# Two-layer hybrid decoder trunk on one core: the mixer's gate, branch, output and recurrence key/query products stream the high and the low input part as one 512-column operand

## The chip, the cores and the metric

The kernel runs on one core of a Trainium2 chip. The metric is device time in microseconds (us). TensorE does matmuls and writes PSUM banks of 128 x 512 float32, of which a core has eight; VectorE (DVE in the profile), ScalarE (ACT) and GpSimd (POOL) do the rest; each works through its own queue in the order in which the program was written for it. The profile gives one execution, engine by engine.

## The reference

Two layers over 256 tokens of width 1024, batch 1, float32. In each layer:

```
x <- x + 1/2 * SwiGLU(RMSNorm(x))
h  = RMSNorm(x);  h @ w_in -> columns for
     A: dilated window attention, 3 head groups merged by softmax-denominator weights
     B: sliding-window grouped-query attention with per-head sinks
     C: gated linear attention (recurrence), with key, query, value, low-rank gate
     G: sigmoid gates, one of width 1024 per branch
x <- x + (sum_i G_i * (branch_i @ w_branch[i])) @ w_out
x <- x + 1/2 * SwiGLU(RMSNorm(x))
```

## The kernel before, in words

**Products.** A float32 product is made of three products of `float32r` parts: weight and input are each split into a high part (a cast) and a low part (the rest), and w_high x_high + w_high x_low + w_low x_high are summed in PSUM. A *unit* is a piece of weights of some 1024 values per partition, as a rule eight 128 x 128 blocks. It arrives by DMA; `emit_split` casts it on ScalarE to `hi` (L191), and VectorE subtracts to get `lo` (L192). `chunk()` hands out the next unit and has the split of the unit four places on written just before; `hi` and `lo` have five buffers each, so the split of unit u+5 waits until TensorE has read unit u.

**Two forms of a feature-major product.** `mm3` makes three matmuls of 256 columns for each block (L331 to L333) into half a PSUM bank. `mmw`, in use in the two SwiGLU halves of a layer, streams high and low input side by side: one 512-column matmul with the high weights for each of the eight blocks (L341), then one 256-column matmul each with the low weights (L343), into a whole bank. `joined` then adds the halves: ScalarE copies the right one to SBUF (`low`, L347), VectorE adds the left (L348).

**The mixer**, stage by stage. (1) *Start*: `tok_proj(272)` makes B's keys and values, into two banks (`psb`). Then come four units by `mm3`: the recurrence's key (two, in one bank) and query (two, in another). Meanwhile `end_norm` turns the sum of squares (L315) by L316 and a power on GpSimd (L256) into the norm's factor `n.r`, spread over partitions by L324; `psb` is read with that factor, and the keys' own norm needs two more powers. (2) Twelve 512-wide `tok_proj` for A, B and C. (3) *Gates*: 24 units by `mm3`, between which `fill()` steps two generators, attention and recurrence. The last big steps of attention are `merge` (three head groups joined; it ends in L781) and B. (4) *Branches*: 12 units by `mm3`, each into one bank, times a gate (L1033), added up (L1035), split to `mh` and `ml` (L1037, L1038). (5) *Output*: 8 units by `mm3`, added to x (L1047).

PSUM has two sets of four banks in rotation: `mm` for these products, `at` for transposes, scores and the norm. `schedule_with_timeline_sim` lets a scheduler decide, before the run, in which order each engine's instructions stand.

Of the kernel before, what the change touches and what calls it, by code (L numbers as in the profile page):

```python
# [17 lines left out]
P = 128  # L18
T = 256
# [52 lines left out]
def trunk_kernel(ctx, tc, x, positions, norm_ffn1, w_ffn1_in, w_ffn1_out, norm_mix, w_in, a_q_norm, a_k_norm,  # L72
# [127 lines left out]
    def chunk():  # L200
        u = cur[0]
        cur[0] += 1
        ahead(u)
        return splits.pop(u)
# [122 lines left out]
        nc.scalar.copy(n.rbc, ps[:, 256:512])  # L327
        yield

    def mm3(ps, wh, wl, xh, xl, first, last):  # L330
        nc.tensor.matmul(ps, wh, xh, start=first, stop=False)  # L331
        nc.tensor.matmul(ps, wh, xl, start=False, stop=False)  # L332
        nc.tensor.matmul(ps, wl, xh, start=False, stop=last)  # L333

    def mmw(ps, w, xhl, first, last):


# [174 lines left out]
    def mixer(l, n, nxt):  # L512
# [32 lines left out]
                    fill()  # L545
            return ps

        def feat_proj(o):
            wh, wl = chunk()
            for k in range(KD):  # L550
                mm3(o, wh[:, k, :], wl[:, k, :], n.h[k], n.l[k], k == 0, k == KD - 1)

        def rope(ps, t, tab, nh):
            C, S = tab
# [148 lines left out]

        yT = [[None] * 4 for _ in range(3)]

        def feature_major(i, y, t):
            pt = turned(y, 4)
            if t == 0:
                yT[i] = [big(F32R), big(F32R), big(F32R), big(F32R)]
            for e in range(2):  # L710
                hv = v3(yT[i][e], 2)[:, :, t * P:(t + 1) * P]
                lv = v3(yT[i][2 + e], 2)[:, :, t * P:(t + 1) * P]
                src = v3(pt[:, e * 256:(e + 1) * 256], 2)
                nc.scalar.copy(hv, src)
                nc.vector.tensor_sub(lv, src, f(hv))


        og = [[None] * NT for _ in range(3)]
# [43 lines left out]
        def merge():  # L762
# [31 lines left out]
            yT[0] = [big(F32R), big(F32R), big(F32R), big(F32R)]  # L794
            for e in range(2):
                nc.scalar.copy(yT[0][e], ysum[e])
                nc.vector.tensor_sub(yT[0][2 + e], ysum[e], f(yT[0][e]))
            yield

        def b_stats(t):  # L800
# [152 lines left out]

        psb = tok_proj(272, 4, True)
        next(fin)
        ps = bank("mm")
        feat_proj(ps[:, 0:T])
        next(fin)
        nc.vector.scalar_tensor_tensor(r64, n.r, 1.0 / HD, n.r, op0=OP.mult, op1=OP.mult)
        nc.vector.tensor_scalar(r8, n.r, 0.125, None, op0=OP.mult)  # L960
# [6 lines left out]
            gt.append(g)  # L967
        bv = v_side(psb, P, P)
        bk = k_rope(psb, tabs[3], 2)
        feat_proj(ps[:, T:2 * T])  # L970
        ck = big()
        nc.vector.tensor_mul(v3(ck, 2), v3(ps, 2), rb2)
        ps = bank("mm")
        for j in range(2):
            feat_proj(ps[:, j * T:(j + 1) * T])
        cq = big()
        nc.vector.scalar_tensor_tensor(v3(cq, 2), v3(ps, 2), HD ** -0.5, rb2, op0=OP.mult, op1=OP.mult)
        bkT = turn_all(bk, 2)
        streams["gla"] = gla(gt, ck, cq)
        streams["att"] = attention()  # L980
# [26 lines left out]

        gates = []
        for c in range(3 * KD // 2):
            ps = bank("mm")  # L1010
            for j in range(2):
                feat_proj(ps[:, j * T:(j + 1) * T])
                fill()
            g = big()
            nc.vector.tensor_mul(v3(g, 2), v3(ps, 2), rb2)
            nc.scalar.activation(g, g, AF.Tanh, scale=0.5)
            gates.append(g)
        while streams:
            for name in list(streams):
                step(name)  # L1020
        mh, ml = [], []
        for mp in range(KD // 2):
            acc = gates[mp]
            for i in range(3):
                wh, wl = chunk()
                ps = bank("mm")
                for j in range(2):
                    for k in range(4):
                        sl = slice((k % 2) * T, (k % 2) * T + T)
                        mm3(ps[:, j * T:(j + 1) * T], wh[:, k, j * P:(j + 1) * P], wl[:, k, j * P:(j + 1) * P],  # L1030
                            yT[i][k // 2][:, sl], yT[i][2 + k // 2][:, sl], k == 0, k == 3)
# [4 lines left out]
            h, lo = big(F32R), big(F32R)  # L1036
            nc.scalar.copy(h, acc)  # L1037
            nc.vector.tensor_sub(lo, acc, f(h))  # L1038
            mh.append(h)
            ml.append(lo)  # L1040
        for m in range(KD):
            wh, wl = chunk()
            ps = bank("mm")
            for k in range(KD):
                sl = slice((k % 2) * T, (k % 2) * T + T)
                mm3(ps[:, 0:T], wh[:, k, :], wl[:, k, :], mh[k // 2][:, sl], ml[k // 2][:, sl], k == 0, k == KD - 1)
            nc.vector.scalar_tensor_tensor(xT[m], ps[:, 0:T], 0.5, xT[m], op0=OP.mult, op1=OP.add)  # L1047
            nxt(m)


# [48 lines left out]
```

## Time and profile before

| | us |
|---|---|
| median of 3 runs (1453.31 to 1454.25) | 1454.0 |
| the profiled execution | 1454.26 |
| its span, first to last instruction | 1452.1 |
| TensorE busy in it | 1440.7 (99%) |
| VectorE busy | 1046.4 (72%) |
| ScalarE busy | 834.6 (57%) |
| GpSimd busy | 127.1 (9%) |

The profiled execution is 2.2 us longer than its span and 0.3 us above the median. A matmul's row shows its way through the array too, so rows of neighbours overlap; what a matmul costs in a stream is the distance from start to start.

### The profile page before, as it was taken

How to read it: one execution, taken by the hardware profiler on the slowest of the kernel's cores; microseconds unless marked ns; L12 is line 12 of the kernel's file. 1: busy time of each engine (PE TensorE's matmuls, PEld its weight loads, DVE VectorE, ACT ScalarE, POOL GpSimd, SP SyncE). 2: the span in 40 equal slices, each digit the busy share in tenths (PEclk: the TensorE clock that was granted, in tenths of full speed). 3: DMA queues.
4: the chain of work that ended last, by engine and by line, in shares of the span. 5: the costliest groups of instructions: out<-in, count | busy, mean ns of one | idle time of the engine just before them, and what ended most of it. 6: DMA issues, size and time to landing. Idle time of an engine off the chain costs nothing.

```text
span 1452.1 us, 23326 instructions
## 1 busy us (share of the span) xinstructions
PE 1440.7 (99%) x9098; PEld 1285.9 (89%) x9098; DVE 1046.4 (72%) x1919; ACT 834.6 (57%) x1436; POOL 127.1 (9%) x108
## 2 busy tenths in 40 slices
PE   8999999999999999999999999999999999999998
PEld 6888898888899998888888888988888999988887
DVE  6887667888677687776677766688766857777753
ACT  6565456556757456565466555466467564566542
POOL 2030012223200000000000000131220000000000
PEclk9999999999999999999999999999999999999999
DMA  9665564443452565655555655643444426565651
GB/s 294 213 198 172 170 212 146 145 145 117 146 174 75 171 220 177 201 177 179 196 194 183 195 168 170 210 152 124 146 145 146 145 88 204 175 203 175 199 182 54
DMA packets 214702, 246.31 MB, mean 170 GB/s; under 512 B 6524, under 2 KB 183376, under 8 KB 214592
## 3 DMA queue, kind: packets, MB, share of 16 engines
q1 hardware_dynamic: 214016, 243.48, 51.4%
q0 software_dynamic: 544, 1.33, 0.4%
q8 instruction: 71, 1.16, 0.3%
q14 instruction: 39, 0.32, 0.1%
q10 hardware_dynamic: 32, 0.01, 0.0%
HBM read 243.76 MB, written 1.05 MB: 169 GB/s over the span
## 4 chain that ended last, share of the span: by engine, by line
PE 95%; DVE 2%; ACT 1%; POOL 1%; DMA 1%; issue 0%; SPq 0%; DVEq 0%
PE p L341 30%; PE p L343 16%; PE p L332 6%; PE p L333 6%; PE p L331 6%; PE p L543 6%; PE p L541 5%; PE p L542 5%; PE p L686 2%; PE p L650 2%; PE p L487 1%; PE p L485 1%; PE p L486 1%; PE p L579 1%; PE p L694 1%; PE p L861 1%
## 5 line engine op out<-in xcount | busy, mean ns | idle before, releaser
L191 ACT CAST hi<-raw 128x1024 fp32r<-128x1024 f32 (+3 forms) x468 | 483.2, 1036 | 489.5 <-PE p L341 271.0
L192 DVE TENSOR_TENSOR lo<-raw,hi 128x1024 fp32r<-128x1024 f32 (+3 forms) x468 | 562.8, 1206 | 266.5 <-ACT hi L191 260.5
L341 PE MATMUL p<-a,hi 128*128 128x512 f32 x1936 | 491.0, 394 | 2.2 <-ACT hi L191 2.1
L341 PEld LDWEIGHTS p<-a,hi 128*128 128x128 f32 x1936 | 348.8, 189 | 65.5 <-ACT hi L191 2.5
L343 PEld LDWEIGHTS p<-a,lo 128*128 128x128 f32 x1936 | 265.4, 190 | 19.3
L343 PE MATMUL p<-a,lo 128*128 128x256 f32 x1936 | 272.1, 282 | 0.0
L333 PE MATMUL p<-a,lo 128*128 128x256 f32 x768 | 218.8, 285 | 0.0
L332 PE MATMUL p<-a,hi 128*128 128x256 f32 x768 | 218.3, 285 | 0.0
L331 PE MATMUL p<-a,hi 128*128 128x256 f32 x768 | 217.7, 285 | 0.0
L256 POOL TENSOR_TENSOR s<-s,neghalf 128x8 f32<-128x8 f32 (+2 forms) x42 | 94.7, 2254 | 1052.6 <-DVE s L316 708.8
L543 PE MATMUL p<-hi,a 128*128 128x512 f32 (+1 forms) x416 | 162.1, 392 | 0.0
L541 PE MATMUL p<-hi,a 128*128 128x512 f32 (+1 forms) x416 | 161.8, 390 | 0.0
L542 PE MATMUL p<-lo,a 128*128 128x512 f32 (+1 forms) x416 | 161.0, 387 | 0.0
L332 PEld LDWEIGHTS p<-a,hi 128*128 128x128 f32 x768 | 147.1, 192 | 0.4
L333 PEld LDWEIGHTS p<-a,lo 128*128 128x128 f32 x768 | 147.1, 191 | 0.2
L331 PEld LDWEIGHTS p<-a,hi 128*128 128x128 f32 x768 | 146.7, 192 | 0.0
L543 PEld LDWEIGHTS p<-hi,a 128*128 128x128 f32 x416 | 79.1, 191 | 15.6
L541 PEld LDWEIGHTS p<-hi,a 128*128 128x128 f32 x416 | 79.4, 191 | 15.0 <-issue 0.7
L542 PEld LDWEIGHTS p<-lo,a 128*128 128x128 f32 x416 | 79.4, 191 | 14.3
L347 ACT COPY low<-p 128x256 f32<-128x256 f32 x200 | 74.5, 373 | 1.2 <-ACT hi L191 0.7
L348 DVE TENSOR_TENSOR w<-p,low 128x256 f32<-128x256 f32 x176 | 73.3, 417 | 0.0
L671 ACT ACTIVATE w<-w,st,s 128x128 f32<-128x128 f32 (+1 forms) x96 | 47.7, 501 | 17.0 <-DVE st L665 17.0
(220 smaller groups left out, 1303.6 us busy)
## 6 DMA issues: line engine op xcount, KB each, us to landing
raw<-in_w_ffn_in_dram SPq DMA_DIRECT2D x87, 1024.0 KB, 5.2
raw<-in_w_in_dram SPq DMA_DIRECT2D x76, 1024.0 KB, 5.0
raw<-in_w_ffn_out_dram SPq DMA_DIRECT2D x34, 1024.0 KB, 5.0
raw<-in_w_branch_dram SPq DMA_DIRECT2D x24, 512.0 KB, 3.5
raw<-in_w_ffn_out_dram SPq DMA_DIRECT2D x12, 768.0 KB, 4.3
raw<-in_w_out_dram SPq DMA_DIRECT2D x8, 1024.0 KB, 5.2
raw<-in_w_in_dram SPq DMA_DIRECT2D x4, 512.0 KB, 3.7
a<-in_x_dram SPq DMA_DIRECT2D x4, 256.0 KB, 5.0
```

Of the source, the lines that this page charges most:

```text
L191: nc.scalar.copy(hi[:, k:k + cut], r[:, k:k + cut])
L192: nc.vector.tensor_sub(lo[:, k:k + cut], r[:, k:k + cut], f(hi[:, k:k + cut]))
L256: nc.gpsimd.tensor_tensor(dst, src, neghalf[:, 0:n], op=OP.pow)
L331: nc.tensor.matmul(ps, wh, xh, start=first, stop=False)
L332: nc.tensor.matmul(ps, wh, xl, start=False, stop=False)
L333: nc.tensor.matmul(ps, wl, xh, start=False, stop=last)
L341: nc.tensor.matmul(ps, wh[:, k, :], xhl[k], start=first and k == 0, stop=False)
L343: nc.tensor.matmul(ps[:, 0:T], wl[:, k, :], xhl[k][:, 0:T], start=False, stop=last and k == nk - 1)
L347: nc.scalar.copy(low, ps[:, T:2 * T])
L541: nc.tensor.matmul(o, xh, wh[:, k - k0, :], start=(k == 0), stop=False)
L542: nc.tensor.matmul(o, xh, wl[:, k - k0, :], start=False, stop=False)
L543: nc.tensor.matmul(o, xl, wh[:, k - k0, :], start=False, stop=(k == KD - 1))
```

## The change

All 96 units that went through `mm3` (48 in each layer) go through `mmw` and `joined`, with a whole bank for each product. Branch inputs `yT` and the merged gates' parts change their layout to [high | low] tiles of one block each, so `feature_major` and the split of the sum make twice as many casts and subtractions, each half as wide. The gate's factor is applied after the joining, in SBUF.

```diff
-    def mm3(ps, wh, wl, xh, xl, first, last):
-        nc.tensor.matmul(ps, wh, xh, start=first, stop=False)
-        nc.tensor.matmul(ps, wh, xl, start=False, stop=False)
-        nc.tensor.matmul(ps, wl, xh, start=False, stop=last)
...
-        def feat_proj(o):
-            wh, wl = chunk()
-            for k in range(KD):
-                mm3(o, wh[:, k, :], wl[:, k, :], n.h[k], n.l[k], k == 0, k == KD - 1)
+        def feat_proj():
+            ps = bank("mm")
+            mmw(ps, chunk(), n.hl, True, True)
+            return ps
...
+        def y_parts(i, e, cols, src):
+
+            for u in range(2):
+                hv, lv = yT[i][2 * e + u][:, 0:T][:, cols], yT[i][2 * e + u][:, T:2 * T][:, cols]
+                nc.scalar.copy(hv, src[:, u])
+                nc.vector.tensor_sub(lv, src[:, u], f(hv))
...
         psb = tok_proj(272, 4, True)
         next(fin)
-        ps = bank("mm")
-        feat_proj(ps[:, 0:T])
+        pk = [feat_proj()]
         next(fin)
...
-        feat_proj(ps[:, T:2 * T])
+        pk.append(feat_proj())
         ck = big()
-        nc.vector.tensor_mul(v3(ck, 2), v3(ps, 2), rb2)
-        ps = bank("mm")
         for j in range(2):
-            feat_proj(ps[:, j * T:(j + 1) * T])
+            joined(ck[:, j * T:(j + 1) * T], pk[j])
+        nc.vector.tensor_mul(v3(ck, 2), v3(ck, 2), rb2)
         cq = big()
...
+        for j in range(2):
+            joined(cq[:, j * T:(j + 1) * T], feat_proj())
...
-            ps = bank("mm")
+            g = big()
             for j in range(2):
-                feat_proj(ps[:, j * T:(j + 1) * T])
+                ps = feat_proj()
                 fill()
-            g = big()
-            nc.vector.tensor_mul(v3(g, 2), v3(ps, 2), rb2)
+                joined(g[:, j * T:(j + 1) * T], ps)
+            nc.vector.tensor_mul(v3(g, 2), v3(g, 2), rb2)
...
-                wh, wl = chunk()
-                ps = bank("mm")
+                w = chunk()
+                o = wrk()
                 for j in range(2):
...
+                    ps = bank("mm")
+                    mmw(ps, [a[:, :, j * P:(j + 1) * P] for a in w], yT[i], True, True)
+                    joined(o[:, j * T:(j + 1) * T], ps)
                 g = gates[i * 4 + mp]
-                nc.vector.scalar_tensor_tensor(g, g, 1.0, ps, op0=OP.add, op1=OP.mult)
+                nc.vector.scalar_tensor_tensor(g, g, 1.0, o, op0=OP.add, op1=OP.mult)
...
         for m in range(KD):
-            wh, wl = chunk()
             ps = bank("mm")
...
+            mmw(ps, chunk(), mhl, True, True)
+            tmp = sm.tile([P, T], F32, tag="res", bufs=2, name=nm("res"))
+            joined(tmp, ps)
+            nc.vector.scalar_tensor_tensor(xT[m], tmp, 0.5, xT[m], op0=OP.mult, op1=OP.add)
```

The lines of the changed file lie five or fewer lower: `mmw` is L336 and L338, `joined` L342 and L343.

**What the scheduler's order becomes: mixer start.** VectorE at the norm of layer 0. `p_2201` holds the sums of squares, L316 makes the power's operand from them, `lo_2214` is the low part of a unit. Before:

```order
L300 TENSOR_TENSOR acc_1666<-acc_1666,sq_2101 128x256
L316 TENSOR_SCALAR s_2202<-p_2201 128x4
L192 TENSOR_TENSOR lo_2214<-raw_2002,hi_2213 128x1024
L192 TENSOR_TENSOR lo_2295<-raw_2002,hi_2294 128x1024
L959 SCALAR_TENSOR_TENSOR s_2132<-s_2208 128x4
```

After the change:

```order
L300 TENSOR_TENSOR acc_1666<-acc_1666,sq_2101 128x256
L192 TENSOR_TENSOR lo_2214<-raw_2002,hi_2213 128x1024
L316 TENSOR_SCALAR s_2202<-p_2201 128x4
L192 TENSOR_TENSOR lo_2288<-raw_2002,hi_2287 128x1024
L192 TENSOR_TENSOR lo_2320<-raw_2024,hi_2319 128x1024
L958 SCALAR_TENSOR_TENSOR s_2132<-s_2208 128x4
```

L316 now stands behind the subtraction of a unit whose split waits for the last matmuls on `psb`. TensorE a little later, with `s_2208` the factor from GpSimd and `p_2316` the bank of the first query product. After the change:

```order
L338 MATMUL p_2286<-a_2098,lo_2065 128x256
L324 MATMUL p_2201<-cst,s_2208 128x128 x2
L336 MATMUL p_2316<-a_1650,hi_2145 128x512
L336 MATMUL p_2316<-a_1661,hi_2145 128x512
L336 MATMUL p_2316<-a_1794,hi_2145 128x512
```

Before the change L324 stood among the first query product's matmuls, and that product had a bank that nobody had used in this mixer. Now `p_2316` is the fifth bank taken, hence the first one of `psb`, and all four units precede any 512-wide `tok_proj`. Ahead of L315, which made the sums, stand the 48 matmuls on `psb`, 15 wide ones and 2 with low weights.

**The merge**, in the gate stage of layer 0. L748 (L749 after the change) is the second transposition of an exchange of statistics, with which the merge begins; `a_3685` (`a_3667` after) is the tile that the first addition of L781 (L782) writes, and the transposition shown is its first reader. TensorE before, where 130 matmuls of 256 columns stand at the three dots:

```order
L748 MATMUL p_4306<-cst,w_4263 128x16 x2
...
L579 MATMUL p_4408<-cst,a_3685 128x128 x4
```

After the change one wide and eight narrow matmuls stand at the first dots and sixteen wide and sixteen narrow ones at the second, 41 in all:

```order
L749 MATMUL p_4272<-cst,w_4229 128x16 x2
...
L338 MATMUL p_4342<-a_2098,lo_4166 128x256
...
L574 MATMUL p_4365<-cst,a_3667 128x128 x4
L574 MATMUL p_4372<-cst,a_3757 128x128 x4
```

The transposition moved up by about five and a half units before to two and a bit now. VectorE's rows between the copy of that exchange and L782 are the ones that it had before, with three splits among them as before, less one gate multiplication.

**Branches to output.** VectorE after the change, at the last branch product: `p_5522` is its bank, `a_5436` to `a_5539` are the last four input tiles of the output product.

```order
L192 TENSOR_TENSOR lo_5546<-raw_5338,hi_5545 128x1024
L1032 SCALAR_TENSOR_TENSOR a_4757<-a_4757,w_5478 128x512
L343 TENSOR_TENSOR w_5509<-p_5522,low_5531 128x256
L1039 TENSOR_TENSOR a_5436<-a_4281,a_5436 128x256
L1039 TENSOR_TENSOR a_5439<-a_4281,a_5439 128x256
L1034 TENSOR_TENSOR a_4384<-a_4384,a_4757 128x512
L1032 SCALAR_TENSOR_TENSOR a_5062<-a_5062,w_5509 128x512
L1034 TENSOR_TENSOR a_4384<-a_4384,a_5062 128x512
L1039 TENSOR_TENSOR a_5536<-a_4384,a_5536 128x256
L1039 TENSOR_TENSOR a_5539<-a_4384,a_5539 128x256
```

TensorE goes from the last branch product at once to the wide matmuls of the first four output products, each with the first four input tiles, then all four with the fifth, sixth, seventh and eighth tile. The fourth product takes the bank `p_5522`. Everywhere outside the four changed stages TensorE's order is what it was.

## Rows read from the trace of the kernel before

**Rows 1.** The page: busy time, share of the span and instructions of each engine; then the shares of the chain that ended last, by engine.

```profile
PE 1440.7 (99%) x9098; PEld 1285.9 (89%) x9098; DVE 1046.4 (72%) x1919; ACT 834.6 (57%) x1436; POOL 127.1 (9%) x108
PE 95%; DVE 2%; ACT 1%; POOL 1%; DMA 1%; issue 0%; SPq 0%; DVEq 0%
```

**Rows 2.** The chain that ended last, in the first SwiGLU: two of its pieces, 30 units apart; start, length, what.

```profile
63.34 1.84 PE p L341 x8
...
147.14 1.84 PE p L341 x8
```

**Rows 3.** Timeline of TensorE in the branch stage: a matmul and the one that stands 24 places (one unit) behind it; start, length.

```profile
519.74 0.28 PE L331 MATMUL p<-a,hi 128*128 128x256 f32 x1
...
522.62 0.28 PE L331 MATMUL p<-a,hi 128*128 128x256 f32 x1
```

**Rows 4.** Timeline of TensorE at the mixer start of layer 0: the first matmul on `psb`, the one behind 36 of these, and the two steps of the norm with what follows.

```profile
200.09 0.29 PE L541 MATMUL p<-hi,a 128*128 128x272 f32 x1
...
204.62 0.28 PE L331 MATMUL p<-a,hi 128*128 128x256 f32 x1
...
208.61 0.42 PE L543 MATMUL p<-hi,a 128*128 128x272 f32 x2
...
208.99 0.97 PE L315 MATMUL p<-ones,acc 128*128 128x1 f32 x8
209.82 0.36 PE L333 MATMUL p<-a,lo 128*128 128x256 f32 x1
...
213.61 0.60 PE L324 MATMUL p<-cst,s 128*128 128x128 f32 x4
```

**Rows 5.** Timelines of VectorE, ScalarE and GpSimd over the same stretch.

```profile
209.99 0.16 DVE L316 TENSOR_SCALAR s<-p 128x4 f32<-128x4 f32 x1 [3.59 <-PE p L315]
...
213.72 0.35 DVE L565 TENSOR_TENSOR w<-p,S 128x64 f32<-128x64 f32 x2
...
216.76 0.48 DVE L606 TENSOR_TENSOR a<-a,s 128x128 f32<-128x128 f32 x2
217.17 0.28 DVE L560 TENSOR_TENSOR a<-p,C 128x128 f32<-128x128 f32 x1
217.37 0.35 DVE L565 TENSOR_TENSOR w<-p,S 128x64 f32<-128x64 f32 x2
```

```profile
209.11 2.00 ACT L191 CAST hi<-raw 128x1024 fp32r<-128x1024 f32 x2 [3.98 <-issue]
```

```profile
210.24 2.08 POOL L256 TENSOR_TENSOR s<-s,neghalf 128x4 f32<-128x4 f32 x1 [107.67 <-DVE s L316]
214.68 1.72 POOL L256 TENSOR_TENSOR s<-s,neghalf 128x2 f32<-128x2 f32 x1 [2.35 <-DVE s L571]
217.60 0.72 POOL L429 TENSOR_TENSOR C<-cosT,hn 128x64 f32<-128x64 f32 x2 [1.20 <-DVE a L560]
...
219.83 0.69 POOL L256 TENSOR_TENSOR s<-s,neghalf 128x2 f32<-128x2 f32 x1
```

**Rows 6.** Timelines at the merge of layer 0: TensorE's two transpositions named above, and VectorE from the copy of the exchange to the two additions of L781.

```profile
416.36 0.29 PE L748 MATMUL p<-cst,w 16*128 16x16 f32 x2
...
432.28 0.60 PE L579 MATMUL p<-cst,a 128*128 128x128 f32 x4
```

```profile
417.36 0.18 DVE L749 COPY st<-p 128x32 f32<-128x32 f32 x1
...
418.67 0.68 DVE L1015 TENSOR_TENSOR a<-p,rbc 128x512 f32<-128x512 f32 x1
419.93 1.23 DVE L192 TENSOR_TENSOR lo<-raw,hi 128x1024 fp32r<-128x1024 f32 x1 [0.58 <-ACT hi L191]
...
428.18 1.29 DVE L781 TENSOR_TENSOR a<-a,a 128x512 f32<-128x512 f32 x2
```

**Rows 7.** Busy time of each engine in the branch stage of layer 0 (us, then PE, PEld, DVE, ACT, POOL, granted clock, DMA share, GB/s), and VectorE's timeline there and where it adds halves.

```profile
488.50:523.00 34.50, 34.50 (x290) 34.50 (x289) 29.03 (x35) 14.99 (x16) 0.00 (x0) 1.00 0.71 229
```

```profile
201.80 0.42 DVE L508 TENSOR_TENSOR xT<-xT,res 128x256 f32<-128x256 f32 x1
202.14 0.42 DVE L348 TENSOR_TENSOR res<-p,low 128x256 f32<-128x256 f32 x1
...
505.90 0.69 DVE L1033 SCALAR_TENSOR_TENSOR a<-a,p 128x512 f32<-128x512 f32 x1 [0.33 <-PE p L333]
506.62 0.69 DVE L1035 TENSOR_TENSOR a<-a,a 128x512 f32<-128x512 f32 x1
507.23 1.22 DVE L192 TENSOR_TENSOR lo<-raw,hi 128x1024 fp32r<-128x1024 f32 x1
508.36 0.68 DVE L1038 TENSOR_TENSOR a<-a,a 128x512 fp32r<-128x512 f32 x1
```

```profile
L347 ACT COPY low<-p 128x256 f32<-128x256 f32 x200 | 74.5, 373 | 1.2 <-ACT hi L191 0.7
```

**Rows 8.** Timeline of TensorE at the kernel's start; and busy time and granted clock (the sixth number behind the stretch) of a stretch there.

```profile
8.97 0.79 PE L341 MATMUL p<-a,hi 128*128 128x512 f32 x1 [2.06 <-ACT hi L191]
...
11.12 2.70 PE L341 MATMUL p<-a,hi 128*128 128x512 f32 x5
13.62 1.05 PE L324 MATMUL p<-cst,s 128*128 128x128 f32 x4
```

```profile
9.00:12.00 3.00, 3.00 (x11) 2.46 (x11) 2.93 (x8) 3.00 (x9) 0.00 (x0) 1.00 1.07 317
```

More of the change, by code (lines that the diff above doesn't have):

```diff
@@ L704, in mixer, with new_y @@
         yT = [[None] * 4 for _ in range(3)]
+        def new_y(i):
+            yT[i] = [big(F32R) for _ in range(4)]
+        def y_parts(i, e, cols, src):
[3 more added lines that the diff above has]
+                nc.vector.tensor_sub(lv, src[:, u], f(hv))
         def feature_major(i, y, t):
@@ L708, in feature_major @@
             if t == 0:
-                yT[i] = [big(F32R), big(F32R), big(F32R), big(F32R)]
+                new_y(i)
             for e in range(2):
[L711 to L715, printed above, removed]
+                y_parts(i, e, slice(t * P, (t + 1) * P), v3(pt[:, e * 256:(e + 1) * 256], 2))
         og = [[None] * NT for _ in range(3)]
@@ L793, in merge @@
                     nc.vector.tensor_add(v, v, v3(pt[:, e * 256:(e + 1) * 256], 2))
-            yT[0] = [big(F32R), big(F32R), big(F32R), big(F32R)]
+            new_y(0)
             for e in range(2):
-                nc.scalar.copy(yT[0][e], ysum[e])
-                nc.vector.tensor_sub(yT[0][2 + e], ysum[e], f(yT[0][e]))
+                y_parts(0, e, slice(0, T), v3(ysum[e], 2))
             yield
@@ L969, in mixer @@
         bk = k_rope(psb, tabs[3], 2)
-        feat_proj(ps[:, T:2 * T])
+        pk.append(feat_proj())
         ck = big()
-        nc.vector.tensor_mul(v3(ck, 2), v3(ps, 2), rb2)
-        ps = bank("mm")
         for j in range(2):
-            feat_proj(ps[:, j * T:(j + 1) * T])
+            joined(ck[:, j * T:(j + 1) * T], pk[j])
+        nc.vector.tensor_mul(v3(ck, 2), v3(ck, 2), rb2)
         cq = big()
-        nc.vector.scalar_tensor_tensor(v3(cq, 2), v3(ps, 2), HD ** -0.5, rb2, op0=OP.mult, op1=OP.mult)
+        for j in range(2):
+            joined(cq[:, j * T:(j + 1) * T], feat_proj())
+        nc.vector.scalar_tensor_tensor(v3(cq, 2), v3(cq, 2), HD ** -0.5, rb2, op0=OP.mult, op1=OP.mult)
         bkT = turn_all(bk, 2)
@@ L1020, in mixer @@
                 step(name)
-        mh, ml = [], []
+        mhl = []
         for mp in range(KD // 2):
@@ L1024, in mixer @@
             for i in range(3):
-                wh, wl = chunk()
-                ps = bank("mm")
+                w = chunk()
+                o = wrk()
                 for j in range(2):
[L1028 to L1031, printed above, removed]
+                    ps = bank("mm")
+                    mmw(ps, [a[:, :, j * P:(j + 1) * P] for a in w], yT[i], True, True)
+                    joined(o[:, j * T:(j + 1) * T], ps)
                 g = gates[i * 4 + mp]
-                nc.vector.scalar_tensor_tensor(g, g, 1.0, ps, op0=OP.add, op1=OP.mult)
+                nc.vector.scalar_tensor_tensor(g, g, 1.0, o, op0=OP.add, op1=OP.mult)
                 if i:
                     nc.vector.tensor_add(acc, acc, g)
[L1036 to L1040, printed above, removed]
+            for j in range(2):
+                hl = big(F32R)
+                a = acc[:, j * T:(j + 1) * T]
+                nc.scalar.copy(hl[:, 0:T], a)
+                nc.vector.tensor_sub(hl[:, T:2 * T], a, f(hl[:, 0:T]))
+                mhl.append(hl)
         for m in range(KD):
-            wh, wl = chunk()
             ps = bank("mm")
[L1044 to L1047, printed above, removed]
+            mmw(ps, chunk(), mhl, True, True)
+            tmp = sm.tile([P, T], F32, tag="res", bufs=2, name=nm("res"))
+            joined(tmp, ps)
+            nc.vector.scalar_tensor_tensor(xT[m], tmp, 0.5, xT[m], op0=OP.mult, op1=OP.add)
             nxt(m)
```

## The prediction

> **What bounds the kernel now.** I read the shares first: TensorE is busy 99% of the span and makes 95% of the chain that ended last [rows 1]. VectorE and ScalarE have room on average. So two things count: how long a unit holds TensorE, and whether TensorE ever waits. In the profile it waits nowhere for long in the four stages; the reader should see that this rests on slack which the order leaves, in microseconds: L324 starts at 213.61 [rows 4], its operand was done at 210.24 + 2.08 = 212.32 [rows 5]; the merge's transposition starts at 432.28, its operand was written by 428.18 + 1.29 = 429.47 at the latest [rows 6].
>
> **The gain per unit.** A matmul's length (0.28 us) says nothing here, since neighbours overlap. By starts, 24 matmuls of a `mm3` unit take 522.62 - 519.74 = 2.88 us, 0.120 each [rows 3]. A `mmw` unit takes (147.14 - 63.34) / 30 = 2.793 us [rows 2], and its eight wide ones 1.84, 0.23 each, so a narrow one 0.119. Both stream 768 columns a block; what goes is one matmul's fixed part of eight units' 24. 0.087 us a unit, 96 units: **-8.4 us**. Weight loads fall from three to two a block, but none shows as a wait today. The bound from below is nothing at all.
>
> Three narrow starts cost 0.360 us where 768 columns at 2.4 GHz need 0.320, 13 ns too much for each matmul [rows 3]. The Trainium skill (TensorE: Matmul & The Clock Gate, section "Wait — 56ns, not 53.3ns?") gives some 2.5 ns as the fixed cost of a warm matmul beyond its columns. By that the 768 matmuls saved would be worth an estimated 1.9 us instead of 8.4, and the sum below would be 6.5 us higher; the trace disagrees, and I go by the rows.
>
> **The added work.** 120 `joined`: a copy of 0.37 us on ScalarE and an addition on VectorE, which follow each other at 0.34 us (201.80 to 202.14) [rows 7]. This lies beside TensorE's work in the gate stage. It is not free where TensorE waits for a step of VectorE's queue. Three places, each once a layer:
>
> **Mixer start.** The old form used four banks before `tok_proj` and L324 fell into a running product. Now L324, the third and the fourth product stand in line behind GpSimd. Step by step in layer 0, with `psb` starting at 200.09: its 48 matmuls at (204.62 - 200.09) / 36 = 0.126 [rows 4], 15 wide at 0.23, 2 narrow: L315 at 209.8 instead of 208.99. The last two on `psb` start at 209.1, half a microsecond later the cast that waited for them (209.11 now, for the last pair from 208.61 on), 1.05 us each (2.00 for two), then the subtraction, 1.13 until the next instruction (507.23 to 508.36) [rows 5, 7]. L316 stands behind it: 211.85 instead of 209.99. GpSimd 0.25 later, 2.08 long: 214.2. TensorE does L315 (0.83, to 209.82 now), the rest of two units (six narrow, one wide, eight narrow: 1.9) and is at L324 at 212.6: **waits 1.6**. L324 takes 0.45. The first `psb` bank is free when L565 has read it, 213.72 + 0.35 = 214.07 now, 1.75 behind the power: 215.95, **waits 1.3**. Product three ends at 218.75. The second power starts 2.36 behind the end of the first and takes 1.72: 218.3; the keys (216.76 + 0.48, 0.84 behind it) are there at 219.15 for a transposition (**0.4**), and the second bank (217.72, 1.32 behind) at 219.6 (**0.25** after the transposition's 0.2). Product four ends at 222.4. In layer 0 GpSimd then makes tables from 0.43 behind L560 on, for 2.23, before the third power (217.60 to 219.83, then 0.69), so the second transposition waits another **0.8**; in layer 1 it has no tables left. 4.35 + 3.55 = **7.9 us**. Bounds: the first wait alone, 1.6 twice; and 6 us a layer, if the tables or a subtraction come between more than once.
>
> **Merge.** From L748 (416.36) to the first of the two L781 (half of 1.29 behind 428.18: 428.85) 12.5 us pass [rows 6]. Less the gate product that is gone from between (0.6), the wait of 0.58, and 0.75 of the 1.0 that the copy came late (it stands right behind a split): 10.6, plus 0.3, since twice two half-size subtractions replace two: 10.9. TensorE's cover was 130 narrow matmuls, 432.28 - 416.36 = 15.9; now it is one wide, eight narrow and two units: 0.23 + 0.95 + 5.59 = 6.8. **Waits 4.1 a layer, 8.2 us.** Behind the transposition in TensorE's queue stand the other transpositions and all products that follow, so nothing fills in; late next are only these. If the three splits in this chain (3 x 1.13) came earlier than they stand, it were 0.7 a layer; if the copy is late as today and ScalarE's part delays more, 5.5.
>
> **Branches to output.** VectorE is busy 29.03 of 34.5 us in the branch stage [rows 7]. Afterwards its work for twelve units is 12 subtractions of 1.13, 24 additions of 0.34, 20 512-wide ones of 0.61 (508.36 less the dependent first: 506.62 to 507.23) and 8 halves of 0.34: 36.5 us, plus 0.1 for each of some ten that depend on the one before (505.90 to 506.62 is 0.72). TensorE needs 12 x 2.79 = 33.5. Up to the last addition VectorE falls about 3.5 us behind; four banks of 1.4 us' work each cover that until the stage's end. The fourth output product wants the last bank 2.8 after the end, the addition is done at 3.9: **1.1**. The last two inputs come through five more steps of VectorE (2.7), a cast and a subtraction (1.0): 7.7; TensorE wants the seventh at 5.5 + 1.1: **1.0**. 2.1 a layer, **4.2 us**; bounds nothing (VectorE not behind) and 4 a layer. The output stage itself needs 1.13 and four 256-wide steps of some 0.34, 2.5 us of VectorE in 2.79, and catches up.
>
> **Sum.** -8.4 + 7.9 + 8.2 + 4.2 = +11.9 on the profiled 1454.26: 1466.2. That execution lies 0.3 above the median, which I neglect. **1466 us.**
>
> **Rivals.** (a) *The products run here as they run in SwiGLU*, where the same scheme with the same four banks goes at 2.793 us for 30 units on end [rows 2]: the steps that I put behind each other overlap with covers that I don't see, at the three places alike. Then the gain stands alone: 1454.3 - 8.4 = 1445.9, faster. It decides from where the waits fall under 5.5 us in all of my 20.3. Against it: SwiGLU has no power from GpSimd and no chain of a dozen VectorE steps in TensorE's way. Chance 0.13. (b) *VectorE is ahead of its line*: splits that stand ahead of L316 and within the merge are done before they hold anything up. Then L316 is 1 us earlier, the merge waits 0.7, the output 0: 5.9 + 1.4 = 7.3 against 8.4, 1453.2, no change. For it: VectorE has 28% free [rows 1]. Against: these splits wait for buffers that TensorE frees just then. Chance 0.08. (c) *The clock falls in the waits.* At the start TensorE waited 2.06 us, and five wide matmuls behind it began 0.50 us apart (11.12 to 13.62) instead of 0.23, although the granted clock is recorded as 1.00 there too, 2.4 GHz [rows 2, 8]. From 8.97 to 13.62 at half the rate is 2.3 us lost. If each merge wait of 4.1 does that, and nothing else, 2 x 2.3 more: 1471; if all six waits do, 1480. The Trainium skill (TensorE: Matmul & The Clock Gate, section "HAM oscillation — how this bites in real kernels") has it that waits between bursts of matmuls put the array back to its low clock, so that the next burst starts slow. No wait of such a length stands in the warm part of this trace; the rows at the start can as well be the first warming. Chance 0.17. My forecast as it stands: 0.62.
>
> **How the numbers follow.** Time 1466, from the likeliest case. By the bounds of the terms that case itself reaches from 3.2 + 1.4 + 0 - 8.4, about as before, to 12 + 11 + 8 - 8.4 = +22.6; taken together they will not all lie at one end, so its own range is 1457 to 1474. (c) adds up to 1480; (b) is left just outside. Range 1455 to 1480: outside lie (a) and most of (b). A difference of 0.2% (2.9 us) is about what a measurement of this kernel can tell from no change. Faster: (a), 0.13. Same: (b) and the low end of the forecast, 0.09. Slower: 0.78.
>
> **What would show it.** In the profile of the changed kernel TensorE's wide and narrow starts 0.23 and 0.119 us apart in the gate stage; idle time before L324 put down to GpSimd's L256 and before L336 in the mixer start put down to VectorE's L560 or L565; before the transposition L574 some 4 us, twice, ended by L782; at the first output products short waits for L343 and L1039. TensorE's busy share falls to about 98%. Wrong it would be if TensorE shows no idle time at L324 or at L574 (then (a)), or if the wide matmuls behind a wait start 0.43 us or more apart (then (c)).

## The result: 1474.6 us, 1.5% slower

| | median us | of the runs |
|---|---|---|
| before | 1453.88 | 1453.31 to 1454.25 |
| changed | 1474.56 | 1473.72 to 1478.12 |

The ratio is 1.0146, with a 95% interval of 1.0134 to 1.0158. The profiled execution of the changed kernel is the longest of its four, 1478.12 us (span 1476.3). The four differ in the granted clock over the whole run: 0.993 in this one, 0.997 in the fastest. That difference will matter.

The page of the changed kernel: busy time and share of the span by engine, then the chain that ended last, by engine. They answer to [rows 1].

```profile
PE 1446.4 (98%) x8330; PEld 1252.0 (85%) x8330; DVE 1084.9 (73%) x2067; ACT 872.2 (59%) x1584; POOL 123.8 (8%) x108
PE 92%; DVE 3%; ACT 1%; POOL 1%; DMA 1%; issue 0%; SPq 0%; DVEq 0%; ACTq 0%; POOLq 0%
```

TensorE's share of the chain fell from 95 to 92%, VectorE's rose from 2 to 3%. What TensorE waited for in the stages that were changed, of the changed kernel (waiting line, releaser: us in total, times, longest):

```profile
PE p L574 <- DVE a L782: 8.3, 2, 4.2
PE p L336 <- DVE w L343: 3.3, 6, 1.0
PE p L324 <- POOL s L256: 2.5, 2, 1.3
PE p L336 <- DVE w L560: 2.3, 2, 1.1
PE p L336 <- DVE a L1039: 0.9, 2, 0.5
PE p L681 <- ACT w L691: 0.6, 2, 0.3
```

These are the places of the prediction, with two exceptions: of the six waits for L343 only the two of 0.96 us stand at the output, the others (0.39 and 0.29 in layer 0) at the seventh and the eighth of the 24 branch products; and the last row is new. TensorE's and VectorE's timelines at the mixer start, the merge and the first outputs of layer 0 (start, length, what, idle time before it and its releaser), against [rows 4 to 6]:

```profile
214.15 0.71 PE L324 MATMUL p<-cst,s 128*128 128x128 f32 x4 [1.28 <-POOL s L256]
215.99 1.82 PE L336 MATMUL p<-a,hi 128*128 128x512 f32 x5 [1.13 <-DVE w L560]
...
421.75 0.19 DVE L750 COPY st<-p 128x32 f32<-128x32 f32 x1 [0.85 <-PE p L749]
432.11 1.29 DVE L782 TENSOR_TENSOR a<-a,a 128x512 f32<-128x512 f32 x2
427.57 1.11 PE L338 MATMUL p<-a,lo 128*128 128x256 f32 x8
432.85 1.97 PE L574 MATMUL p<-cst,a 128*128 128x128 f32 x8 [4.17 <-DVE a L782]
...
537.71 3.04 PE L336 MATMUL p<-a,hi 128*128 128x512 f32 x12 [0.96 <-DVE w L343]
541.20 0.50 PE L336 MATMUL p<-a,hi 128*128 128x512 f32 x1 [0.46 <-DVE a L1039]
```

From VectorE's copy at 421.75 to the first half of L782 at 432.75 are 11.0 us. TensorE had covered 6.8 of them and stood still. The second cost shows in the granted clock. Busy time by stretch (us; PE, PEld, DVE, ACT, POOL, granted clock, DMA share, GB/s), of the changed kernel:

```profile
205.00:212.00 7.00, 7.00 (x47) 6.35 (x46) 2.72 (x6) 2.47 (x5) 0.00 (x0) 1.00 0.44 150
212.00:216.00 4.00, 1.60 (x13) 1.22 (x11) 3.25 (x11) 2.90 (x10) 1.96 (x1) 1.00 0.41 102
216.00:220.00 4.00, 4.00 (x14) 3.38 (x15) 2.07 (x12) 0.82 (x1) 2.35 (x6) 0.59 0.42 162
428.00:433.00 5.00, 0.83 (x7) 0.63 (x6) 5.00 (x12) 0.98 (x2) 0.00 (x0) 0.88 0.65 210
433.00:440.00 7.00, 7.00 (x38) 6.96 (x39) 2.73 (x7) 2.73 (x7) 0.00 (x0) 0.60 0.00 0
```

Right behind the waits TensorE is busy all the time at 0.59 and 0.60 of its clock, between the two levels of 1.2 and 2.4 GHz. Five wide matmuls take 1.82 us from 215.99 on, and the eight 128-column products of L574 take 1.97; e3 below has the same rows without the slow clock.

By stage (each from TensorE's first start in it to its first start in the next; layer 0 / layer 1):

| | before | changed | difference |
|---|---|---|---|
| mixer start | 19.0 / 19.0 | 23.6 / 24.8 | +4.6 / +5.8 |
| token-major products | 176.0 / 176.0 | 175.5 / 175.5 | -0.5 / -0.5 |
| gates | 93.3 / 93.3 | 99.5 / 98.2 | +6.2 / +4.9 |
| branches | 34.6 / 34.6 | 35.1 / 35.1 | +0.5 / +0.5 |
| output | 23.0 / 23.0 | 24.35 / 24.35 | +1.3 / +1.3 |

Together that is 24.1 of the 24.2 us by which the span grew.

### The profile page after: what moved, and what is told of

It reads as the page before. It is cut to its first block, busy times and chain, and to the rows that moved or that the text cites. A ratio compares the mean times of both kernels' runs of the same rounds, so it can differ in the third digit from the quotient of the medians.

```text
span 1476.3 us, 22149 instructions
## 1 busy us (share of the span) xinstructions
PE 1446.4 (98%) x8330; PEld 1252.0 (85%) x8330; DVE 1084.9 (73%) x2067; ACT 872.2 (59%) x1584; POOL 123.8 (8%) x108
## 4 chain that ended last, share of the span: by engine, by line
PE 92%; DVE 3%; ACT 1%; POOL 1%; DMA 1%; issue 0%; SPq 0%; DVEq 0%; ACTq 0%; POOLq 0%
PE p L336 41%; PE p L338 22%; PE p L538 5%; PE p L536 5%; PE p L537 5%; PE p L681 2%; PE p L645 2%; PE p L574 1%; PE p L482 1%; PE p L481 1%; PE p L480 1%; PE p L861 1%; PE p L689 1%; POOL s L256 1%; DVE lo L192 1%; DMA raw<-in_w_ffn_in_dram 1%
## 5 line engine op out<-in xcount | busy, mean ns | idle before, releaser
L191 ACT CAST hi<-raw 128x1024 fp32r<-128x1024 f32 (+3 forms) x468 | 484.4, 1038 | 442.4 <-PE p L336 328.6
L336 PE MATMUL p<-a,hi 128*128 128x512 f32 x2704 | 697.0, 396 | 9.3 <-DVE w L343 3.3
L336 PEld LDWEIGHTS p<-a,hi 128*128 128x128 f32 x2704 | 485.8, 190 | 100.1 <-DVE w L343 5.7
L338 PEld LDWEIGHTS p<-a,lo 128*128 128x128 f32 x2704 | 375.3, 191 | 29.1
L338 PE MATMUL p<-a,lo 128*128 128x256 f32 x2704 | 386.6, 283 | 0.0
L342 ACT COPY low<-p 128x256 f32<-128x256 f32 x320 | 118.5, 372 | 26.9 <-PE p L338 15.0
L343 DVE TENSOR_TENSOR w<-p,low 128x256 f32<-128x256 f32 x224 | 93.0, 418 | 0.1
L681 PEld LDWEIGHTS p<-a,w 128*128 128x128 f32 x320 | 39.4, 191 | 2.6 <-ACT w L691 1.0
L681 PE MATMUL p<-a,w 128*128 128x64 f32 x320 | 40.5, 271 | 0.6 <-ACT w L691 0.6
L653 DVE CUSTOM_DVE_ANT_0 w<-p,cst 128x128 f32<-128x128 f32 (+1 forms) x128 | 32.9, 319 | 7.8 <-PE p L645 7.8
L480 PE MATMUL p<-hi,a 128*128 128x512 f32 x88 | 34.2, 389 | 0.0
L481 PE MATMUL p<-lo,a 128*128 128x512 f32 x88 | 34.2, 389 | 0.0
L482 PE MATMUL p<-hi,a 128*128 128x512 f32 x88 | 34.2, 389 | 0.0
```

The source lines that it names most:

```text
L191: nc.scalar.copy(hi[:, k:k + cut], r[:, k:k + cut])
L336: nc.tensor.matmul(ps, wh[:, k, :], xhl[k], start=first and k == 0, stop=False)
L338: nc.tensor.matmul(ps[:, 0:T], wl[:, k, :], xhl[k][:, 0:T], start=False, stop=last and k == nk - 1)
L342: nc.scalar.copy(low, ps[:, T:2 * T])
L343: nc.vector.tensor_add(dst, ps[:, 0:T], low)
L480: nc.tensor.matmul(pss[t], a, wh[:, k - k0, :], start=(k == 0), stop=False)
```

## The experiments

Theory: at the mixer start and at the merge TensorE waits, and each wait is followed by a stretch at a lower clock; joins keep VectorE late around the branches. Rivals: the slow stretches have another cause; a wait taken away comes back elsewhere. e1 to e5 start from the changed kernel. A start is called late by as much as it comes after the place that the undisturbed distance from the start before gives it; that is a little more than the idle time in the row (4.33 us for 4.17 at the merge). Medians in us, ratio to before with its 95% interval:

| | edit | median | ratio |
|---|---|---|---|
| e1 | merge one step later | 1473.22 | 1.0137 [1.0120, 1.0154] |
| e2 | two start products in other banks | 1467.73 | 1.0097 [1.0082, 1.0112] |
| e3 | the merge's wait filled with matmuls | 1469.54 | 1.0110 [1.0095, 1.0125] |
| e4 | branches in the old form | 1469.47 | 1.0110 [1.0095, 1.0125] |
| e5 | merge's step moved, stream's end kept | 1468.18 | 1.0101 [1.0088, 1.0115] |
| e6 | e2 + e4 + e5 | 1455.59 | 1.0014 [1.0005, 1.0022] |
| e7 | e6, gates' multiplication on GpSimd | 1453.79 | 0.9999 [0.9990, 1.0008] |
| e8 | new form at start (as e2) and output only | 1452.93 | 0.9993 [0.9984, 1.0001] |
| e9 | e7, joins ahead of the streams' step | 1451.09 | 0.9980 [0.9971, 0.9989] |
| e10 | e7, another step of the merge taken out | 1451.49 | 0.9983 [0.9974, 0.9992] |

### e3: the wait filled with work

```diff
+            pw = bank("at")
+            for i in range(17):
+                nc.tensor.matmul(pw, n.h[0][:, 0:P], n.hl[0], start=(i == 0), stop=(i == 16))
             ysum = [big(), big()]
```

> Seventeen wide matmuls whose result nobody reads, 0.23 us each, 3.9 us together, stand in TensorE's queue ahead of the merge's transposition, in the stretch in which it stood idle for 4.33 us. Nothing is taken away. Theory (idle time costs its own length and then a stretch at half clock): the idle time at L574 shrinks to about 0.4 us and is replaced by work of the same length; the granted clock then stays at 1.00 behind it, and 2.84 us in layer 0 and 1.5 in layer 1 come back: 4.3 us off the profiled 1478.1, 2 to 5 off the median of 1474.6, so 1470 to 1473. Rival 1 (the slow stretch behind the merge is not caused by the idle time): 1474.6 to 1475.5, with a clock of 0.6 behind the merge as before. Rival 2 (the added matmuls come where TensorE is not idle): 2 x 3.9 us slower, 1482.

Measured 1469.54: 5.0 us less than the changed kernel, with 7.8 us more work. TensorE's timeline at the merge and at the mixer start, and the same two stretches as above, of e3:

```profile
421.30 4.04 PE L786 MATMUL p<-a 128*128 128x512 f32 x17
430.74 1.04 PE L574 MATMUL p<-cst,a 128*128 128x128 f32 x8
...
214.02 0.71 PE L324 MATMUL p<-cst,s 128*128 128x128 f32 x4 [1.28 <-POOL s L256]
215.85 1.39 PE L336 MATMUL p<-a,hi 128*128 128x512 f32 x5 [1.12 <-DVE w L560]
428.00:433.00 5.00, 5.00 (x38) 4.66 (x38) 4.97 (x8) 3.16 (x8) 0.00 (x0) 1.00 0.37 103
433.00:440.00 7.00, 7.00 (x48) 6.21 (x47) 5.89 (x15) 5.16 (x11) 1.01 (x1) 1.00 0.22 77
```

The same eight products that took 1.97 us take 1.04, the clock is 1.00, and the gate stage is 96.2 us in both layers instead of 99.5 and 98.2. So the slow stretch belongs to the idle time: idling for 4.2 us cost more than useless work of that length. At the mixer start the waits are the same, 1.28 and 1.12, but this time five wide matmuls behind them took 1.39 us instead of 1.82: there the clock did not fall in this execution.

### e2: other banks for two start products

```diff
-        def feat_proj():
-            ps = bank("mm")
+        def feat_proj(tag="mm"):
+            ps = bank(tag)
...
-            joined(cq[:, j * T:(j + 1) * T], feat_proj())
+            joined(cq[:, j * T:(j + 1) * T], feat_proj("at"))
```

> The third and the fourth recurrence product go to banks of the attention's four, which are free at that time, instead of the products' four. So neither waits until GpSimd's power has let L560 and L565 read the two banks of psb, and L324 stands by the instruction order thirteen wide and eight narrow matmuls later. Theory (two waits and a stretch of half clock, each once a layer): in the trace of the change L324 is 1.44 us late, the first matmul on psb's bank 1.3 us, and the stretch behind it loses 1.9 us in layer 0 and 3.1 us in layer 1; all of it goes, 2 x 2.7 + 5.0 = 10.4 us off the profiled 1478.1, 7 to 10 off the median of 1474.6: 1464 to 1467, with a granted clock of 1.00 over the mixer start. Rival 1 (the bank is not what holds the line; GpSimd's powers are): L324 or the transposition of the keys waits instead, 0 to 3 us off, 1472 to 1475. Rival 2 (the wait alone costs): 5.4 us off, 1469, with the clock falling as before.

Measured 1467.73, 6.8 less: just short of the theory's 7 to 10. The theory was priced from the profiled execution; whether the others of the changed kernel lose less at the start, no trace shows. Two stretches at the mixer start and two at the merge, of e2:

```profile
212.00:216.00 4.00, 4.00 (x23) 3.46 (x23) 3.24 (x12) 3.18 (x10) 1.65 (x2) 1.00 0.55 171
216.00:221.00 5.00, 5.00 (x29) 4.36 (x28) 3.92 (x11) 1.42 (x2) 3.80 (x6) 1.00 0.76 258
...
423.00:428.00 5.00, 0.84 (x7) 0.64 (x7) 5.00 (x12) 1.01 (x2) 0.00 (x0) 0.92 0.67 210
428.00:435.00 7.00, 7.00 (x44) 6.70 (x45) 4.18 (x12) 3.38 (x10) 0.25 (x1) 0.81 0.00 0
```

No wait is left at the start, and the stage takes 18.6 us in both layers (19.0 before). The untouched merge behaves as it did.

### e1 and e5: cover for the merge

e1 puts one step of the streams (one gate unit) between the additions and the transpositions:

```diff
-            yield
+            for _ in range(2):
+                yield
             ysum = [big(), big()]
```

> The merge takes one step more before its transpositions, so that by the instruction order four units and sixteen 128-column products stand between L749's exchange and the first of them, where two units stood. Nothing else is meant to change. Theory (the wait and a stretch of half clock behind it, each once a layer): in the trace of the change TensorE's start of the transposition L574 is 4.33 us late in both layers, and the starts behind it are another 2.84 us late in layer 0 (granted clock 0.60 from 433 to 440 us) and 1.5 us in layer 1. All of it goes: 2 x 4.33 + 2.84 + 1.5 = 13.0 us off the profiled 1478.1; off the median of 1474.6, whose runs show a clock of 0.995 to 0.997 instead of 0.993, some 9 to 13, so 1462 to 1466, and a clock of 1.00 in the window of the merge. Rival 1 (the wait alone costs; the slow stretch belongs to something else): 8.7 us off, 1466, and the granted clock around the merge falls as before. Rival 2 (the wait moves to the next step of the merge, since VectorE is what is late): 0 to 3 us off, 1472 to 1475, with a new wait of some 4 us at a later transposition.

Measured 1473.22, only 1.3 less. The wait at L574 is gone and the clock is 1.00, but others stand in its place. What TensorE waited for between 425 and 499 us, of e1:

```profile
PE p L336 <- DVE a L709: 1.7, 1, 1.7
PE p L336 <- DVE a L343: 1.0, 1, 1.0
PE p L336 <- ACT hi L191: 0.2, 1, 0.2
```

The expectation failed, and its second rival was nearer, though with another line: an early branch product waits 1.7 us for the last input part (L709), since every later step of that stream came a unit later. Another cost, 2.0 us a layer, shows as no wait. Attention's 48 score products of the gate stage stand in TensorE's queue in a row of 24, one of 8 and one of 16 in the changed kernel, and in one of 16 and four of 8 in e1. TensorE's first row of them in the changed kernel, and two rows of e1:

```profile
450.85 2.05 PE L645 MATMUL p<-a,a 64*128 64x128 f32 x24
...
444.65 1.16 PE L645 MATMUL p<-a,a 64*128 64x128 f32 x16
448.54 1.16 PE L645 MATMUL p<-a,a 64*128 64x128 f32 x8
```

Eight of them take as long as sixteen here. From start to start, the way into these rows, through them and out of them adds up to 6.8 us a layer in e1 and 4.8 in the changed kernel. In e5 the step between the merge's two groups of transpositions is taken out in exchange, so that the stream ends where it ended:

```diff
             yield
+            yield
             ysum = [big(), big()]
...
                     nc.scalar.copy(v3(ysum[e], 2)[:, :, t:T:2], v3(pt[:, e * 256:(e + 1) * 256], 2))
-            yield
             for t in range(NT):
```

> As in e1 the merge takes one step more before its transpositions, but the step that stood between its two groups of transpositions is gone, so the steps behind it stand where they stood in the change, the last transposition ahead of the branch products too. In e1 the gate stage was 95.5 us (99.5 and 98.2 in the change), but the branch stage waited 1.84 us for the last input part (L709), and 0.41 and 1.24 us came in the gate stage. Theory (queue positions: the branch stage waited because the step came later): the 1.84 us go in both layers and the branch stage is 35.1 us again; 1473.2 - 2 x 1.84 = 1469.5, or less. Rival (VectorE has no room in the gate stage: whatever the wait at the transposition gave it to catch up must be waited for somewhere): 1472 to 1475, with waits for VectorE of about 3.5 us a layer at other places of the gate and branch stages.

Measured 1468.18: the theory. The branch stage is 35.0 us (37.3 in e1). In the gate stage some 3 us of late starts a layer stay, 2.0 of them now at the row of seven transpositions (28 products of L574), where TensorE waits 1.4 us for a bank. Behind that wait the clock stayed at 1.00 in layer 0; in layer 1 it fell, and the gate stage is 96.7 us there instead of 95.1. A stretch of layer 1, of e5:

```profile
1162.00:1166.00 4.00, 3.78 (x11) 3.01 (x12) 3.50 (x11) 2.64 (x9) 0.00 (x0) 0.57 0.35 122
```

### e4: branches in the old form

The function `mm3` is back for these products:

```diff
-                o = wrk()
+                o = bank("mm")
                 for j in range(2):
-                    ps = bank("mm")
-                    mmw(ps, [a[:, :, j * P:(j + 1) * P] for a in w], yT[i], True, True)
-                    joined(o[:, j * T:(j + 1) * T], ps)
+                    for k in range(4):
+                        mm3(o[:, j * T:(j + 1) * T], w[0][:, k, j * P:(j + 1) * P], w[1][:, k, j * P:(j + 1) * P],
+                            yT[i][k][:, 0:T], yT[i][k][:, T:2 * T], k == 0, k == 3)
```

> Only the branch products go back to the old form (three 256-column matmuls a block, one bank for two units, no joining); gates, output and mixer start stay in the new one. It gives back the gain of 24 units a layer: 2 x 24 x 0.087 = 4.2 us slower by the sum in the prediction. Theory (VectorE falls behind by the joins of the branch stage): the late starts at the stage's first products (0.55 and 0.45 us) and at the output's (1.12 for the bank, 0.61 for the input tile), 2.7 us a layer, go: 5.5 off, net 1.3 off, 1473. Rival 1 (the output's waits come from its own joins and splits): the last 1.7 a layer stay, net 2.2 slower, 1477. Rival 2 (the gain of a unit is smaller than 0.087, about 0.02 by the Trainium skill's 2.5 ns a matmul): then only 1.0 is given back and 1470 comes out.

Measured 1469.47, 5.1 less, below all three. The late starts go, as the theory has it: branches 34.55 us, output 22.3, together 2.55 a layer less. But the old form gives back only 0.9 us a layer, not 2.1 as I wrote, for I had charged 24 units a layer where there are 12. The price of a unit holds: where nothing waits, a branch product (half a unit) of the changed kernel starts 1.40 us after the one before, 2.80 a unit, and the stage's 35.1 us hold 1.5 of late starts. The number of the second rival, 1470, came out without its reason. A branch product of the changed kernel and the first row of the next:

```profile
519.80 1.09 PE L336 MATMUL p<-a,hi 128*128 128x512 f32 x4
...
521.20 0.63 PE L336 MATMUL p<-a,hi 128*128 128x512 f32 x2
```

The output's low time also shows that its waits came from the branch stage.

### e6 to e10: together, and what was left

> The three edits together: the attention's banks for two of the start's products (as in e2), the branch products in the old form (as in e4), the merge's step moved (as in e5); gates, output and mixer start keep the new form. Theory (each place has its own price and they add): by stage against the kernel before, from the runs so far: mixer start and token-major stage -0.3 us a layer, gates 95.5 - 93.3 = +2.2 at the most, branches 0, output 22.31 - 23.04 = -0.7; together +1.2 a layer, 1453.6 + 2.4 = 1456, or down to 1453 if the gate stage waits less than in e1. Rival (waits taken away in one place come back behind it): above 1459.

e6: 1455.59, the prices add. The gate stage is 95.1 us with 3.0 of late starts. TensorE's timeline at the merge, of e6:

```profile
432.79 1.91 PE L579 MATMUL p<-cst,a 128*128 128x128 f32 x16
436.14 0.63 PE L579 MATMUL p<-cst,w 128*128 128x128 f32 x4 [1.44 <-DVE a L799]
```

The transposition that follows the merge's waits for a bank that VectorE's additions (L799) free late. In this execution the clock stayed at 1.00 behind it. e7 takes 0.69 us per gate off VectorE:

```diff
-            nc.vector.tensor_mul(v3(g, 2), v3(g, 2), rb2)
+            nc.gpsimd.tensor_mul(v3(g, 2), v3(g, 2), rb2)
```

> As e6, and the gates' multiplication by the norm's row (512 columns, 0.69 us of VectorE, twelve a layer) is done by GpSimd, which is idle 92% of the span; an estimate of 1.8 us each from its 0.50 us for 64 columns and 0.69 for 128. It takes 8 us a layer off VectorE in the gate stage and adds a join's worth to nothing else. Theory (what is left of waits in the gate stage is VectorE's lack of room): the remaining 0.4 and 1.2 us go, 2 to 3 us below e6. Rival 1 (what waits there is a position in the queue, not room): same as e6 within 1 us. Rival 2 (GpSimd and VectorE hold each other up): VectorE's instructions beside it get longer than 0.41, 0.69 and 1.21 us, and it is slower than e6.

e7: 1453.79, 1.8 less than e6, just short of the theory's 2 to 3; the wait at L799 went from 1.4 to 0.8. But the second rival is there too. GpSimd's new line and VectorE's splits beside it in e7, and those splits in e6 (count, busy, mean ns), 395 to 490 us:

```profile
L1020 POOL TENSOR_TENSOR a<-a,rbc 128x512 f32<-128x512 f32 x11 | 15.1, 1375 | 83.0 <-DVE a L348 73.4 <-DVE s L810 6.8 <-DVE s L813 2.8
L192 DVE TENSOR_TENSOR lo<-raw,hi 128x1024 fp32r<-128x1024 f32 x27 | 35.9, 1343 | 18.7 <-ACT hi L191 16.7 <-ACT a L713 1.6 <-PE p L343 0.3
```

```profile
L192 DVE TENSOR_TENSOR lo<-raw,hi 128x1024 fp32r<-128x1024 f32 x26 | 31.5, 1221 | 15.8 <-ACT hi L191 15.7
```

A split takes 1343 ns instead of 1221 on average: of the 7.6 us that left VectorE some 3.3 came back in its splits (27 x 0.12). The cause shows row by row: the six splits that overlap a GpSimd multiplication took 1.77 us on average (1.21 to 2.24), the other 21 1.22. e9 puts each join ahead of the streams' step:

```diff
             for j in range(2):
-                ps = feat_proj()
+                joined(g[:, j * T:(j + 1) * T], feat_proj())
                 fill()
-                joined(g[:, j * T:(j + 1) * T], ps)
```

> As e7, and each gate's join stands ahead of the streams' step in the code instead of behind it, so that by the instruction order the seven transpositions of the merge, which stood in one row, are spread over two units, the first ten matmuls later. In e7 the gate stage was 94.4 us with 2.3 us late: 0.44 and 0.42 us at two places and 0.92 and 0.52 in that row of transpositions (L799's bank, then the weights' split). Theory (what waits in that row is the row itself: four banks, emptied by additions): 0.92 and 0.52 go, 1.4 a layer, 1453.8 - 2.9 = 1450.9. Rival (a join earlier in VectorE's queue makes something else late): 1453 to 1456.

e9: 1451.09, as the theory has it, 0.20% below the kernel before. No wait for VectorE is left in the four stages (the branches are in the old form); what TensorE waited for, of e9, from the longest on:

```profile
PE p L260 <- DMA cst<-in_const_dram: 3.0, 1, 3.0
PE p L341 <- ACT hi L191: 1.6, 3, 1.1
PE p L357 <- DMA a<-in_x_dram: 1.5, 1, 1.5
PE p L579 <- DVE a L599: 0.6, 2, 0.3
```

The first three rows stand at the kernel's start, but for two waits of 0.3 for L191 in the gates; the last stands in the token-major products. The gates take 93.0 us, the branches 34.6, the output 22.3 (93.3, 34.6 and 23.0 before). e10 instead puts the step between the merge's two groups back and takes out the last `yield` of the merge.

> As e7, but the step between the two groups of the merge's transpositions is back, and the step behind the second group is taken out instead. By the instruction order six transpositions still stand in a row, but the scores of the next group stand a unit later. Theory (the row waits for banks): part of the 0.92 and 0.52 us goes, 1452 to 1453.5. Rival (the step behind the second group now holds up the stream's end and the branches wait as in e1): 1455 to 1457.

e10: 1451.49, a little better than the theory. e8, with gates and branches in the old form, was the control:

> Gates and branches in the old form; mixer start (with the attention's banks as in e2) and output in the new one. Theory (only stages in which VectorE has room keep the gain): gates and branches 93.3 and 34.6 us as before, output 22.31 instead of 23.04, mixer start 0.3 less: 1453.6 - 2 x 1.0 = 1451.6. Rival 1 (the output's low time in e4 came from the stages ahead of it, not from its own form): 1453. Rival 2 (the merge waits even so, since the order around it has moved): 1458 to 1465.

e8: 1452.93; its interval reaches 1.0001. The output is 22.3 us as expected, but the gates take 94.0 us in the old form instead of 93.3, with no single start over 0.25 us late. The difference lies at the score products of e1's kind. TensorE's second row of them before, and what stands in its place in e8:

```profile
451.61 2.05 PE L650 MATMUL p<-a,a 64*128 64x128 f32 x24
...
451.72 1.16 PE L650 MATMUL p<-a,a 64*128 64x128 f32 x8
453.12 1.49 PE L650 MATMUL p<-a,a 64*128 64x128 f32 x16
```

The row is cut in two. Start to start these products take 4.4 us a layer before, 5.2 in e8, 5.0 in e9 and 4.5 in e10; all else in e8's gate stage is as before within 0.15 us.

## Why the prediction was right in its sign and short in its size

The kernel is slower, by waits at the places named; 1474.6 lies within 1455 to 1480. But the likeliest value, 1466, was 8.6 us short. Term by term:

- **Gain, -8.4.** The price of a unit was right: an undisturbed one takes 2.80 us in the gate stage (from 399.24 to 402.04) and in the branches, against 2.88. Where nothing waits, the new form saves 0.7 us a layer in the output (22.3, e4), 0.3 from the mixer start to the end of the token-major products (e2), 0.9 in the branches (35.1 less 1.5 late) and 1.8 in the gates (e9: 93.0, of which 0.9 late and 0.6 more at the score products): 3.7 a layer, **-7.4**. The Trainium skill (TensorE: Matmul & The Clock Gate, section "Wait — 56ns, not 53.3ns?") would have given an estimated 1.9; the runs are nearer to the rows.
- **Mixer start, +7.9.** The first two waits were right: 1.28 us for GpSimd's power (I had 1.6) and 1.13 for the bank (1.3). With the clock at 1.00 the stage takes 22.0 us in e3, +3.0 a layer, of which the token-major products give back 0.5. The two starts are 1.44 and 1.29 late, **+5.4** for both layers. The three waits behind (0.4, 0.25, 0.8) did not come. The failing step is the second power: it takes 0.70 us in the changed kernel, not the 1.72 of [rows 5], and the tables ahead of the third power take 1.25, not 2.23. So the keys and the second bank are ready a microsecond earlier, and the second transposition's input too; in e3, at full clock, none of the three is waited for. GpSimd's timeline in the changed kernel:

```profile
216.45 0.70 POOL L256 TENSOR_TENSOR s<-s,neghalf 128x2 f32<-128x2 f32 x1 [2.35 <-DVE s L566]
218.34 0.72 POOL L424 TENSOR_TENSOR C<-cosT,hn 128x64 f32<-128x64 f32 x2 [1.20 <-DVE a L555]
...
219.59 0.69 POOL L256 TENSOR_TENSOR s<-s,neghalf 128x2 f32<-128x2 f32 x1
```

- **Merge, +8.2.** Right: 4.17 us of idle time twice, 8.3 (starts 4.33 late, **+8.6**). The chain took 11.0 us (10.9), the cover 6.8.
- **Branches to output, +4.2.** The bank was right (1.1; its start was 1.12 late), the input tile costs 0.61 of the 1.0. Not seen: 0.55 and 0.45 us at the seventh and the eighth branch product, and starts of some 0.1 us around all of these, 0.7 together. 3.4 a layer, **+6.8**, and not the output's fault, as e4 shows. That this excess over the forecast is as large as what the mixer start came short by is luck.
- **Not in the sum: the rest of the gate stage.** A start that waits for ScalarE's L691 is 0.44 late, and the score products take 0.4 more than before (4.8 against 4.4): **+1.7** for both layers.
- **The clock.** The likeliest value put it at nothing. This is the larger step that failed, and it was rival (c). Late starts at half rate behind the waits come to 1.6 and 2.8 us at the two mixer starts and 2.8 and 1.5 at the two merges in the profiled execution, **+8.7**; by estimate about 5 in the median run, which is 3.6 us shorter than the profiled one at a clock of 0.995. (c) gave 1471 for the merges alone and 1480 for all six waits. I gave it 0.17, because no warm wait of such a length stood in the trace before, and the rows at the kernel's start [rows 8] could be the first warming. That (c)'s price, 2.3 us a wait, came near the 1.4 to 2.8 lost at each merge is partly luck: the trace of the kernel before keeps no record of the granted clock ahead of 14.85 us, and the view shows 1.00 where there is none. So the 1.00 in [rows 8] is no reading, and those rows may show a clock that had not yet risen. The Trainium skill (TensorE: Matmul & The Clock Gate, section "HAM oscillation — how this bites in real kernels") has the next burst of matmuls start slow behind a wait; at the six merges with a wait of 4.2 us the traces agree.

Added up, -7.4 + 5.4 + 8.6 + 6.8 + 1.7 + 8.7 = 23.8 of the 24.2 us by which the profiled span grew.

Rivals (a) and (b) fall with the waits. What I did not foresee at all came out in e1: the wait at the merge also stood ahead of later deadlines, and a step put in for it cut up the rows of score products, so taking it away alone gave 1.3 us.

What stays open: why the waits of 1.1 to 1.4 us, at the mixer start and at the row of transpositions, lowered the clock in some cases only.

## What to carry to other kernels

When a scheme that works in one stage is carried to others, price each stage by what the other engines must do between its products, and add to a new wait of TensorE the slow stretch that can follow it. A step moved to give cover moves everything behind it in its stream: move a later step back by as much, and look at the stage that reads the stream's end and at what the step does to rows of small products. Bring each stage over by itself; here e9, with the new form in three of the four stages, is 3 us (0.2%) ahead of the kernel before, where the same idea in all four lost 21.

## What the runs showed of the hardware

- All six merges with a wait of 4.2 us (two each in the changed kernel, e2 and e4) were followed by half-rate starts. Behind the two waits of 1.3 and 1.1 us at the mixer start this was so in three of ten cases (both of the changed kernel, one of two in e1, none in e3, e4 and e5), and behind the wait of 1.4 us at the row of transpositions in one of four (layer 1 of e5; not its layer 0, nor e6). Two stretches behind a merge in e4, one in each layer:

```profile
431.00:437.00 6.00, 5.75 (x30) 5.75 (x31) 2.16 (x5) 2.52 (x7) 0.00 (x0) 0.55 0.01 2
1155.00:1161.00 6.00, 5.71 (x31) 5.71 (x32) 2.23 (x6) 2.69 (x7) 0.00 (x0) 0.58 0.01 4
```

- VectorE's splits, which read two operands from SBUF, took 1.77 us on average where they overlapped GpSimd's multiplication of 512 columns (six of them in e7) and 1.22 elsewhere. The additions of L348, which read one operand from PSUM, took 0.42 us in both cases (three and 20 of them).
- Eight 64-row score products in a row of their own took 1.16 us, sixteen 1.16 or 1.49 and 24 2.05 (e1, e8): where a row is cut matters.
